# Latent attention in another order: compressed queries ahead of keys and values, V copied out in wider pieces

## The chip, the cores and the metric

The kernel runs on one core of one Trainium2 chip. The metric is device time in microseconds (us), the median over timed runs of the whole program. Five engines work side by side, each from a queue that it runs strictly in order: TensorE (PE, products; its weight loads are PEld), VectorE (DVE), ScalarE (ACT), GpSimd (POOL) and SyncE (SP, which here only issues DMAs). They meet at semaphores.

## What is computed

Two decoder layers over 512 tokens of width 1024: forgetting attention ("fox") with a feed-forward block, then multi-head latent attention ("MLA") with another. The change lies in the second attention and in how both attentions store V. Cut to what matters:

```python
def mla_shared_kv(h, positions, kv_norm, w_kv_a, ckv_norm, w_uk, w_uv):
    hn = rmsnorm(h, kv_norm)
    a = hn @ w_kv_a                                   # 1024 -> 256 + 32
    c_kv = rmsnorm(a[..., :KV_RANK], ckv_norm)
    k_rope = rope(a[..., KV_RANK:][:, :, None, :], positions)
    k_nope = jnp.einsum('bsr,rhd->bshd', c_kv, w_uk)  # 256 -> 16 heads x 64
    v = jnp.einsum('bsr,rhd->bshd', c_kv, w_uv)
    ...
def mla_attention(xn, positions, k, v, w_dq, cq_norm, w_uq, w_o):
    c_q = rmsnorm(xn @ w_dq, cq_norm)                 # 1024 -> 768
    q = (c_q @ w_uq).reshape(B, S, MLA_HEADS, MLA_NOPE + MLA_ROPE)
    q = jnp.concatenate([q[..., :MLA_NOPE], rope(q[..., MLA_NOPE:], positions)], axis=-1)
    o = causal_block_attention(q, k, v, 1.0 / math.sqrt(MLA_NOPE + MLA_ROPE))
    return o.reshape(B, S, MLA_HEADS * MLA_V) @ w_o
```

## The kernel before

Every matrix product is made to fp32 accuracy from two halves: an operand is split into a high part (ACT copies it to a rounded type) and a low part (DVE subtracts), and three products hi·hi, hi·lo, lo·hi are summed in PSUM (`mm3`, L356 to L359). Weights come by DMA into two stage buffers, and ACT (L101 or L110) and DVE (L102 or L111) split them one step ahead of use. `specs` lists the weights in the order in which `getw` asks for them; those named in `ACT_QUEUE` (`uk`, `uq`, `uv`) are loaded from ACT's queue, the rest from SP's. Activations lie with features on partitions and the 512 tokens along the free dimension; a PSUM bank holds 128 x 512.

The MLA stage (L851 on) first makes `kva` (keys' and values' compressed form, token by token, L862 to L873), then the row of inverse norms `hrow`, then six units `dq` (compressed queries, L921 to L932; after the second of them `feature_major` transposes `kro` and `ckv`, L893). L1018 to L1028 prepare the first pair of heads. A k unit is 6 products (`uk`, L941), a query unit 18 (`uq`, L968: the plain ones, L988, and the rotary one that four heads share, L1000), a v unit 24 products of 256 columns (`uv`). Before, their order is: k unit 0, first half of the rotary unit, the queries' norm row `qrow`, by which the rotary tables `rope_s` and `rope_c` are multiplied (L1023, L1024), second half, plain unit 0, `to_heads(0)`, v unit 0, plain unit 1. `to_heads` (L958) and the k unit write the heads' operands by SP's DMAs into one of three tiles `mqk`: part 0 the query's hi and lo (L966), part 3 the rotary query (L965), parts 1 and 2 the key (L955, 512 KB a head); `kr` holds the rotary key (L917).

`attention` then runs 16 heads in a pipeline: score products of the next head (L407, three passes), transposes of the probabilities (L436), softmax (L420 to L430), "fill" steps that prepare later heads, and the product with V (L450). `v_unit` (L505) holds two token blocks of V in a PSUM bank and copies each out in pieces of one block and two heads, 128 x 128, ACT the hi part (L540, fox L545), DVE the lo part (L541, fox L546).

What stands in the code is not yet the queues' order: at build time a scheduler with its own estimate of durations places the instructions on each engine, and the engines keep to it.

Of the kernel before, what the change touches and what calls it, by code (L numbers as in the profile page):

```python
# [56 lines left out]
def yoco_fox_mla_kernel(  # L57
# [152 lines left out]
    def gcol(base):  # L210
        return lambda k: gain_t[:, base + k:base + k + 1]

    G_ATTN, G_FFN, G_KV, G_CKV, G_CQ = 0, 16, 32, 40, 42

    for hf in range(2):
        spec(("kva", hf), [(0, (4, KVR + ROPE), kslice(w_kv_a, 0, KVR + ROPE, 4 * hf, 4 * hf + 4))],
             gained(4, KVR + ROPE, gcol(G_KV + 4 * hf)))
    for m in range(QT):
        spec_cols(("dq", m), mla_w_dq[0], m * P, gain=gcol(G_ATTN + 8))
# [4 lines left out]
    def spec_uk(pp):  # L224
        spec_cols(("uk", pp), uk_f, pp * P, nk=2)
# [9 lines left out]

    spec_uk(0)
    spec_uq(0)
# [267 lines left out]
    def v_unit(key, src, nk, halves, V, new_v, col, extra=None):  # L505
# [6 lines left out]
        def go(hf, ks, b):  # L512
# [21 lines left out]
            if hf == halves - 1 and (extra or off == 256):  # L534
                for bb in ([b] if extra else [b - 1, b]):
                    tt, oo = st[bb]
                    for pr in range(2):
                        pv = tt[:, oo + pr * P:oo + (pr + 1) * P].rearrange("p (h d) -> p h d", h=2)
                        if col is None:
                            ACT.copy(out=V[pr][:, bb, :, 0:64], in_=pv)  # L540
                            DVE.tensor_tensor(out=V[pr][:, bb, :, 64:128], in0=pv,  # L541
                                              in1=V[pr].bitcast(F32)[:, bb, :, 0:64], op=ALU.subtract)
                        else:
                            c = col[:, bb:bb + 1]
                            ACT.activation(out=V[pr][:, bb, :, 0:64], in_=pv, func=AF.Copy, scale=c)  # L545
                            DVE.scalar_tensor_tensor(out=V[pr][:, bb, :, 64:128], in0=pv, scalar=c,  # L546
                                                     in1=V[pr].bitcast(F32)[:, bb, :, 0:64],
                                                     op0=ALU.mult, op1=ALU.subtract)
                    if extra:
                        extra(bb, tt[:, 256:272])  # L550
# [54 lines left out]
    with ExitStack() as fx:  # L605
# [18 lines left out]
        def vtiles():  # L624
            return [fpool.tile([P, NB, 2, P], F32R, name="v", tag="v", bufs=4) for _ in range(2)]
# [112 lines left out]
        def fox_passes(n):  # L738
# [4 lines left out]
                  lambda n: (lambda kb: vts[n // 4][n // 2 % 2][:, kb, n % 2, :]), oT, fills)  # L743
# [107 lines left out]
    with ExitStack() as fx:  # L851
# [9 lines left out]

        kvb = [dense_bank() for _ in range(NB)]  # L862
        for hf in range(2):
            w = getw(("kva", hf))
            wh, wl = kview(w[0], KVR + ROPE), kview(w[1], KVR + ROPE)
            for b in range(NB):
                o = kvb[b][:, 0:KVR + ROPE]
                for i in range(4):
                    xh = xs[:, 0, 4 * hf + i, b * P:(b + 1) * P]
                    xl = xs[:, 1, 4 * hf + i, b * P:(b + 1) * P]  # L870
                    PE.matmul(o, lhsT=xh, rhs=wh[:, i, :], start=(hf == 0 and i == 0), stop=False)
                    PE.matmul(o, lhsT=xh, rhs=wl[:, i, :], start=False, stop=False)
                    PE.matmul(o, lhsT=xl, rhs=wh[:, i, :], start=False, stop=(hf == 1 and i == 3))  # L873
            if hf == 0:
                hcol = rms.finish()
        hrow = to_row(hcol)
# [16 lines left out]
        def feature_major():  # L893
# [10 lines left out]
            rope_keys(krf)  # L904

        def rope_keys(krf):
# [6 lines left out]
            krs = mp.tile([P, 2, S], F32R, name="krs", tag="rr", bufs=1)  # L913
            ACT.copy(out=krs[r, 0, :], in_=krf[r])
            DVE.tensor_tensor(out=krs[r, 1, :], in0=krf[r], in1=krs.bitcast(F32)[r, 0, :], op=ALU.subtract)
            for q in range(2):
                SP.dma_start(out=kr.bitcast(F32)[q * 64:(q + 1) * 64, :],  # L917
                             in_=krs.bitcast(F32)[r, q:q + 1, :].broadcast_to([ROPE, 2, S]))


        for m in range(QT):  # L921
            w = getw(("dq", m))
            o = dense_bank()
            dense(o, w, xs, range(KT), True, True)
            if m == 0:
                rq = Rms(QT, QR)
            if m == 1:
                feature_major()
            c = tmp_tile("cq")
            DVE.tensor_tensor(out=c, in0=o, in1=hrow, op=ALU.mult)  # L930
            gained_split(cc, m, c, gcol(G_CQ)(m))
            rq.add(c)  # L932
# [5 lines left out]
        def mbank(name):  # L938
            return bank(early.pop(0) if early else ps_mm, name)

# [59 lines left out]
        def rope_unit(qd):  # L1000
            def done(o):
                raw = tmp_tile("qr")
                ACT.copy(out=raw, in_=o)
# [15 lines left out]
        rope0 = rope_unit(0)  # L1019
        run(k_unit(0) + rope0[:1])  # L1020
        qrow = to_row(rq.finish(), -QW ** -0.5)
        state["qrow"] = qrow
        DVE.tensor_tensor(out=rope_s, in0=rope_s, in1=qrow, op=ALU.mult)  # L1023
        DVE.tensor_tensor(out=rope_c, in0=rope_c, in1=qrow, op=ALU.mult)  # L1024
        run(rope0[1:])
        run(nope_unit(0, 0))
        to_heads(0)
        run(uv_unit(0, vts[0]) + nope_unit(0, 1))  # L1028
# [143 lines left out]
```

## Time and profile before

| | us |
|---|---|
| timed runs (median of 3; lowest, highest) | 1243.5 (1242.1, 1244.34) |
| the profiled execution, its own time | 1242.24 |
| its span, first to last instruction | 1240.5 |
| TensorE busy, share of the span | 1215.9, 98% |
| VectorE busy, share of the span | 720.0, 58% |

The profile is that of one execution: its page, and views asked of its trace (stretches with each engine's busy time, engines in order of time, who waited for whom). A busy PE is read with care, since its products are pipelined: what tells is the distance from one start to the next, and the gaps. All times inside the trace count from the span's start.

### The profile page before, as it was taken

The numbers are of one execution on the slowest core, as the hardware profiler recorded it, in microseconds if no ns is written. First come the engines' busy times: TensorE is split into PE (matmuls) and PEld (weight loads), VectorE is DVE, ScalarE is ACT, GpSimd is POOL, SyncE is SP. The second block draws the span as 40 slices with busy tenths as digits, with TensorE's granted clock in tenths as the row PEclk, the third lists the DMA queues.
The fourth block names the chain that finished last, engine by engine and source line by source line (L and its number), as shares of the span: only waits on it lengthen the run. The fifth ranks groups of instructions, "written<-read, shape, count | busy, mean of one in ns | idle before, by whom it ended". The sixth has DMA issues, their size and how long they took to land. (4 is left out here: it accounts for less than half of the span.)

```text
span 1240.5 us, 16569 instructions
## 1 busy us (share of the span) xinstructions
PE 1215.9 (98%) x5963; PEld 1023.5 (83%) x5963; DVE 720.0 (58%) x1525; ACT 537.8 (43%) x1188; POOL 245.1 (20%) x277
## 2 busy tenths in 40 slices
PE   8999999999999999999999899999999999999997
PEld 7878888888888888888898788888888888888886
DVE  5776777755455545633367789876545455552323
ACT  6555565543323323323364467665423333232322
POOL 3333332211111111000012133333011111110101
PEclk9999999999999999999999999999999999999999
DMA  5555455142332333333324675634233323332232
GB/s 173 142 144 140 115 129 136 52 118 86 102 101 87 102 95 90 104 106 95 102 86 105 155 186 147 167 102 135 85 100 88 102 85 102 89 98 102 85 104 84
DMA packets 193396, 137.24 MB, mean 111 GB/s; under 512 B 5937, under 2 KB 174945, under 8 KB 193313
## 3 DMA queue, kind: packets, MB, share of 16 engines
q1 hardware_dynamic: 186208, 128.55, 37.7%
q10 hardware_dynamic: 7104, 7.63, 2.1%
q8 instruction: 47, 0.77, 0.3%
q14 instruction: 37, 0.30, 0.1%
HBM read 104.30 MB, written 2.10 MB: 86 GB/s over the span
## 5 line engine op out<-in xcount | busy, mean ns | idle before, releaser
L101 ACT CAST whi<-wstage 128x512 fp32r<-128x512 f32 (+4 forms) x386 | 215.7, 603 | 464.5 <-PE dn L358 296.7
L102 DVE TENSOR_TENSOR wlo<-wstage,whi 128x512 fp32r<-128x512 f32 x366 | 282.6, 806 | 117.6 <-ACT whi L101 117.4
L357 PE MATMUL dn<-xs,whi 128*128 128x512 f32 x704 | 275.0, 391 | 0.0
L359 PE MATMUL dn<-xs,wlo 128*128 128x512 f32 x704 | 274.1, 389 | 0.0
L358 PE MATMUL dn<-xs,whi 128*128 128x512 f32 x704 | 274.0, 389 | 0.0
L359 PEld LDWEIGHTS dn<-xs,wlo 128*128 128x128 f32 x704 | 132.2, 188 | 27.4
L357 PEld LDWEIGHTS dn<-xs,whi 128*128 128x128 f32 x704 | 132.2, 188 | 27.2
L358 PEld LDWEIGHTS dn<-xs,whi 128*128 128x128 f32 x704 | 132.2, 188 | 27.1
L781 POOL TENSOR_TENSOR u<-u,g 128x512 f32<-128x512 f32 x44 | 68.7, 1562 | 425.0 <-DVE u L780 379.6
L780 DVE TENSOR_TENSOR u<-dn,inv_row 128x512 f32<-128x512 f32 x44 | 30.4, 691 | 146.8 <-PE dn L359 146.8
L427 POOL TENSOR_SCALAR p<-p,rs 128x128 f32<-128x128 f32 (+1 forms) x128 | 63.8, 507 | 136.1 <-DVE rs L424 134.3
L422 ACT ACTIVATE p<-s,nm 128x256 f32<-128x256 f32 (+3 forms) x128 | 67.4, 544 | 22.1 <-DVE nm L420 19.2
L420 DVE CUSTOM_DVE_ANT_0 s<-s,mask 128x256 f32<-128x256 f32 (+3 forms) x128 | 61.1, 495 | 16.1 <-PE s L407 16.1
L777 DVE TENSOR_TENSOR g<-dn,inv_row 128x512 f32<-128x512 f32 x44 | 30.4, 691 | 68.8 <-PE dn L359 68.8
L321 POOL TENSOR_TENSOR acc<-acc,sq 128x512 f32<-128x512 f32 x22 | 35.4, 1610 | 161.8 <-ACT sq L320 161.7
L441 DVE TENSOR_TENSOR pt<-t,pt 128x384 fp32r<-128x384 f32 (+1 forms) x96 | 52.6, 591 | 3.3 <-ACT pt L440 2.5
L440 ACT CAST pt<-t 128x384 fp32r<-128x384 f32 (+1 forms) x96 | 45.0, 524 | 18.5 <-PE t L436 17.2
L436 PE MATMUL t<-ident,p 128*128 128x128 f32 x320 | 44.6, 275 | 6.9 <-DVE oraw L454 6.6
L357 PE MATMUL qkp<-xs_fox,whi 128*128 128x512 f32 x128 | 51.2, 400 | 0.0
L358 PE MATMUL qkp<-xs_fox,whi 128*128 128x512 f32 x128 | 50.3, 393 | 0.0
L436 PEld LDWEIGHTS t<-ident,p 128*128 128x128 f32 x320 | 36.4, 140 | 16.8 <-DVE oraw L454 9.0
L359 PE MATMUL qkp<-xs_fox,wlo 128*128 128x512 f32 x128 | 50.1, 392 | 0.0
(290 smaller groups left out, 2346.7 us busy)
## 6 DMA issues: line engine op xcount, KB each, us to landing
wstage<-in_w_gate SPq DMA_DIRECT2D x44, 512.0 KB
wstage<-in_w_up SPq DMA_DIRECT2D x44, 512.0 KB
wstage<-in_w_down SPq DMA_DIRECT2D x30, 512.0 KB
wstage<-in_fox_w_in SPq DMA_DIRECT2D x22, 512.0 KB
qk<-hl SPq DMA_DIRECT2D x32, 256.0 KB
mqk<-hl SPq DMA_DIRECT2D x16, 512.0 KB
wstage<-in_w_down SPq DMA_DIRECT2D x16, 448.0 KB
wstage<-in_mla_w_uq ACTq DMA_DIRECT2D x8, 576.0 KB
```

Source lines behind the costliest of these rows:

```text
L101: ACT.copy(out=hi[:, a:b], in_=stage[:, a:b])
L102: (POOL if shared and a else DVE).tensor_tensor(out=lo[:, a:b], in0=stage[:, a:b], in1=hi.bitcast(F32)[:, a:b], op=ALU.subtract)
L357: PE.matmul(o, lhsT=wh, rhs=xh, start=start, stop=False)
L358: PE.matmul(o, lhsT=wh, rhs=xl, start=False, stop=False)
L359: PE.matmul(o, lhsT=wl, rhs=xh, start=False, stop=stop)
L420: DVE.tensor_tensor_reduce(out=sv, in0=sv, in1=mask[:, S - n:S], scale=1.0, scalar=BIG, op0=ALU.add, op1=ALU.min, accum_out=nm[:, qb:qb + 1])
L422: ACT.activation(out=pv, in_=sv, func=AF.Exp, bias=nm[:, qb:qb + 1], scale=-1.0, accum_out=ssum[:, qb:qb + 1])
L427: POOL.tensor_scalar(out=pv[:, :cut], in0=pv[:, :cut], scalar1=r, scalar2=1.0, op0=ALU.mult, op1=ALU.mult)
L436: PE.transpose(t[:, i * P:(i + 1) * P], self.p[:, POFF[qb] + kb * P:POFF[qb] + (kb + 1) * P], ident)
L440: ACT.copy(out=self.pt[0][:, sl], in_=t[:, :n])
L441: DVE.tensor_tensor(out=self.pt[1][:, sl], in0=t[:, :n], in1=self.pt[0].bitcast(F32)[:, sl], op=ALU.subtract)
L781: POOL.tensor_tensor(out=u, in0=u, in1=g, op=ALU.mult)
```

## The change

Five edits. (1) The six `dq` units come ahead of `kva`; the first two wait for `hrow` and are copied out together. (2) The queries' norm is taken between the halves of `kva`, and its row `qrow` behind them. (3) The first plain unit and the rotary unit come next, then `to_heads(0)`, then `feature_major`, the second plain unit, the k unit and the v unit. The rotary unit of the first four heads multiplies by `qrow` itself; the tables are multiplied by `qrow` later (`rope_rows`), behind the rotary key, for the other units. (4) The hi and lo of the rotary key lie in two tiles of the `tmp` pool. (5) V is copied out in pieces of 256 columns: in MLA two token blocks of two heads, in fox one block of four heads, whose tile now holds four heads.

```diff
+    for m in range(QT):
+        spec_cols(("dq", m), mla_w_dq[0], m * P, gain=gcol(G_ATTN + 8))
     for hf in range(2):
         spec(("kva", hf), ...
-    for m in range(QT):
-        spec_cols(("dq", m), mla_w_dq[0], m * P, gain=gcol(G_ATTN + 8))
...
+    spec_uq(0)
     spec_uk(0)
-    spec_uq(0)
     spec_uv(0)
...
+                if col is None:
+                    for pr in range(2):
+                        pv = t.rearrange("p (b r h d) -> p r b h d", b=2, r=2, h=2)[:, pr]
+                        bs = slice(b - 1, b + 1)
+                        ACT.copy(out=V[pr][:, bs, :, 0:64], in_=pv)
+                        DVE.tensor_tensor(out=V[pr][:, bs, :, 64:128], in0=pv,
+                                          in1=V[pr].bitcast(F32)[:, bs, :, 0:64], op=ALU.subtract)
...
+            rope_rows()
+
+        def rope_rows():
+            DVE.tensor_tensor(out=rope_s, in0=rope_s, in1=state["qrow"], op=ALU.mult)
+            DVE.tensor_tensor(out=rope_c, in0=rope_c, in1=state["qrow"], op=ALU.mult)
...
-        rope0 = rope_unit(0)
-        run(k_unit(0) + rope0[:1])
-        qrow = to_row(rq.finish(), -QW ** -0.5)
-        state["qrow"] = qrow
-        DVE.tensor_tensor(out=rope_s, in0=rope_s, in1=qrow, op=ALU.mult)
-        DVE.tensor_tensor(out=rope_c, in0=rope_c, in1=qrow, op=ALU.mult)
-        run(rope0[1:])
-        run(nope_unit(0, 0))
+        run(nope_unit(0, 0) + rope_unit(0))
         to_heads(0)
-        run(uv_unit(0, vts[0]) + nope_unit(0, 1))
+        feature_major()
+        run(nope_unit(0, 1) + k_unit(0) + uv_unit(0, vts[0]))
```

The queues that this makes differ most just ahead of the first head's scores. On VectorE, before, from the rotary product by `rope_c` (L1007) to the second plain query (the last `qf`); `rr` is the rotary query, `mv` V, `wlo` the low half of a weight, here of later units:

```order
L1007 TENSOR_TENSOR qr<-qr,rope_c 128x512
L993 TENSOR_TENSOR qf<-uq,inv_row 128x512
L1008 TENSOR_TENSOR qr<-qr,sw 128x512
L996 TENSOR_TENSOR hl<-qf,hl 128x512
L1011 TENSOR_TENSOR rr<-qr,rr 128x512
L541 TENSOR_TENSOR mv<-vv,mv 128x2x64
L102 TENSOR_TENSOR wlo<-wstage,whi 128x256
L541 TENSOR_TENSOR mv<-vv,mv 128x2x64 x4
L102 TENSOR_TENSOR wlo<-wstage,whi 128x512
L541 TENSOR_TENSOR mv<-vv,mv 128x2x64 x2
L993 TENSOR_TENSOR qf<-uq,inv_row 128x512
```

And now, from the rotary key's product (`krf`) to the first copies of V; `hl<-uk,hl` is the low half of the first key, the 128x512 piece of `wlo` that of `uv`'s weights:

```order
L939 TENSOR_TENSOR krf<-krf,rope_c 32x512
L1030 TENSOR_TENSOR rr<-qr,rr 128x512
L940 TENSOR_TENSOR krf<-krf,sw 32x512
L931 TENSOR_TENSOR rope_s<-rope_s,inv_row 128x512
L932 TENSOR_TENSOR rope_c<-rope_c,inv_row 128x512
L943 TENSOR_TENSOR krs<-krf,krs 32x512
L1009 TENSOR_TENSOR qf<-uq,inv_row 128x512
L102 TENSOR_TENSOR wlo<-wstage,whi 128x512
L102 TENSOR_TENSOR wlo<-wstage,whi 128x256
L1012 TENSOR_TENSOR hl<-qf,hl 128x512
L966 TENSOR_TENSOR hl<-uk,hl 128x512
L541 TENSOR_TENSOR mv<-vv,mv 128x4x64 x3
```

What moved: the key's low half, before done long ago, is now the last of eleven rows that begin with the rotary key, and the split of `uv`'s weights stands behind the second plain query.

The rows of VectorE just ahead of these, now, from the rotary query's product by `qrow` (`qr<-uq`):

```order
L1020 TENSOR_TENSOR qr<-uq,inv_row 128x512
L1024 STREAM_SHUFFLE sw<-qr 128x512
L937 STREAM_SHUFFLE sw<-krf 32x512
L1026 TENSOR_TENSOR qr<-qr,rope_c 128x512
L377 SCALAR_TENSOR_TENSOR cc<-ct,gain_t,cc 128x512
L1027 TENSOR_TENSOR qr<-qr,sw 128x512
L377 SCALAR_TENSOR_TENSOR cc<-ct,gain_t,cc 128x512
```

Rotary query, rotary key and the compressed keys (`cc<-ct`) now take turns here; before, the last two were done between the `dq` units.

SP's queue of DMAs up to the first head, before:

```order
L917 DMA kr<-krs 64x1x512 x2
L955 DMA mqk_5398<-hl 128x1x1024
L955 DMA mqk_5399<-hl 128x1x1024
L966 DMA mqk_5398<-hl 128x1x512
L965 DMA mqk_5398<-rr 64x1x512 x2
L965 DMA mqk_5399<-rr 64x1x512 x2
```

and now:

```order
L982 DMA mqk_5370<-hl 128x1x512
L982 DMA mqk_5371<-hl 128x1x512
L981 DMA mqk_5370<-rr 64x1x512 x2
L981 DMA mqk_5371<-rr 64x1x512 x2
L945 DMA kr<-krs 64x1x512 x2
L981 DMA mqk_5372<-rr 64x1x512
L971 DMA mqk_5370<-hl 128x1x1024
L971 DMA mqk_5371<-hl 128x1x1024
```

What moved: the key's copies (1024 columns) went from ahead of the query's to behind them and behind `kr`.

## Rows read from the trace of the kernel before

**Rows 1.** The page: busy time, share of the span and instructions of TensorE.

```profile
PE 1215.9 (98%) x5963; PEld 1023.5 (83%) x5963; DVE 720.0 (58%) x1525; ACT 537.8 (43%) x1188; POOL 245.1 (20%) x277
```

**Rows 2.** Stretches: length, busy time per engine, PE clock (1.00 full), DMA share, GB/s.

```profile
679.00:686.00 7.00, 7.00 (x46) 6.28 (x45) 5.86 (x9) 2.29 (x5) 1.67 (x1) 1.00 0.60 176
...
689.30:692.60 3.30, 0.36 (x3) 0.18 (x3) 0.68 (x1) 0.39 (x1) 0.00 (x0) 1.00 1.05 319
692.60:695.80 3.20, 3.20 (x11) 2.91 (x12) 1.75 (x7) 2.34 (x7) 0.00 (x0) 0.51 0.44 110
695.80:700.00 4.20, 4.20 (x22) 3.43 (x21) 2.96 (x14) 2.13 (x8) 2.10 (x4) 0.97 0.42 93
```

**Rows 3.** PE in order of time: start, duration, instruction, [idle before <- releaser].

```profile
689.14 0.51 PE L407 MATMUL s<-mqk 128*128 128x256 f32 x2
692.58 0.47 PE L407 MATMUL s<-kr,mqk 128*128 128x256 f32 x1 [2.94 <-DMA mqk<-rr]
692.85 0.63 PE L407 MATMUL s<-mqk 128*128 128x256 f32 x2
693.28 0.41 PE L407 MATMUL s<-kr,mqk 128*128 128x256 f32 x1
...
695.74 0.56 PE L357 MATMUL uk<-cc,whi 128*128 128x512 f32 x1
```

**Rows 4.** Waits of PE, 600 to 860 us: total, times, longest.

```profile
PE s L407 <- DMA mqk<-rr: 2.9, 1, 2.9
PE t L436 <- DVE oraw L454: 1.8, 2, 0.9
PE uk L357 <- DVE mv L541: 1.6, 2, 0.8
PE o L450 <- DVE pt L441: 1.2, 1, 1.2
```

**Rows 5.** PE in order of time, a query unit's end and the v unit.

```profile
681.65 0.39 PE L358 MATMUL uq<-cc,whi 128*128 128x512 f32 x1
681.88 0.39 PE L359 MATMUL uq<-cc,wlo 128*128 128x512 f32 x1
682.11 0.28 PE L531 MATMUL vv<-whi,cc 128*128 128x256 f32 x1
682.22 0.28 PE L532 MATMUL vv<-wlo,cc 128*128 128x256 f32 x1
...
684.98 0.40 PE L357 MATMUL uq<-cc,whi 128*128 128x512 f32 x1
```

**Rows 6.** DVE in order of time.

```profile
680.41 0.69 DVE L1023 TENSOR_TENSOR rope_s<-rope_s,inv_row 128x512 f32<-128x512 f32 x1 [1.02 <-ACT inv_row L352]
681.02 0.68 DVE L1024 TENSOR_TENSOR rope_c<-rope_c,inv_row 128x512 f32<-128x512 f32 x1
681.74 1.67 DVE L1007 TENSOR_TENSOR qr<-qr,rope_c 128x512 f32<-128x512 f32 x1
...
686.10 0.41 DVE L102 TENSOR_TENSOR wlo<-wstage,whi 128x256 fp32r<-128x256 f32 x1
```

**Rows 7.** POOL in order of time: the rotary products.

```profile
650.10 1.29 POOL L910 TENSOR_TENSOR sw<-sw,rope_s 32x512 f32<-32x512 f32 x1 [6.54 <-DVE sw L909]
...
681.18 1.67 POOL L1006 TENSOR_TENSOR sw<-sw,rope_s 128x512 f32<-128x512 f32 x1 [11.72 <-DVE rope_s L1023]
```

**Rows 8.** SP and ACT in order of time: DMA issues.

```profile
685.41 0.52 SPq L966 DMA_DIRECT2D mqk<-hl  x1
686.03 1.29 SPq L965 DMA_DIRECT2D mqk<-rr  x2
...
686.55 0.37 ACTq L137 DMA_DIRECT2D wstage<-in_mla_w_uq  x1
```

**Rows 9.** Stretches around DMAs: columns as in rows 2.

```profile
676.00:679.00 3.00, 3.00 (x15) 2.45 (x14) 2.66 (x15) 0.59 (x1) 0.00 (x0) 1.00 1.00 180
...
685.40:686.50 1.10, 1.10 (x6) 0.89 (x6) 1.10 (x3) 0.61 (x4) 0.00 (x0) 1.00 0.00 0
...
688.50:691.00 2.50, 1.14 (x6) 0.58 (x4) 1.23 (x4) 0.47 (x2) 0.00 (x0) 1.00 0.98 325
```

**Rows 10.** Copies of MLA's V: count, duration in ns (lowest/median/highest).

```profile
L541 DVE TENSOR_TENSOR mv<-vv,mv x32: 271/282/292, 685.9 to 812.9; 128x128 fp32r<-128x128 f32 x32
```

**Rows 11.** Waits of PE, 0 to 270 us (the fox attention): total, times, longest.

```profile
PE t L436 <- DVE oraw L454: 4.8, 8, 0.9
```

More of the change, by code (lines that the diff above doesn't have):

```diff
@@ L534, in go @@
             if hf == halves - 1 and (extra or off == 256):
-                for bb in ([b] if extra else [b - 1, b]):
-                    tt, oo = st[bb]
[L537 to L548, printed above, removed]
+                if col is None:
[5 more added lines that the diff above has]
+                                          in1=V[pr].bitcast(F32)[:, bs, :, 0:64], op=ALU.subtract)
+                for bb in ([] if col is None else [b] if extra else [b - 1, b]):
+                    tt, oo = st[bb]
+                    pv = tt[:, oo:oo + 256].rearrange("p (h d) -> p h d", h=4)
+                    c = col[:, bb:bb + 1]
+                    ACT.activation(out=V[0][:, bb, :, 0:64], in_=pv, func=AF.Copy, scale=c)
+                    DVE.scalar_tensor_tensor(out=V[0][:, bb, :, 64:128], in0=pv, scalar=c,
+                                             in1=V[0].bitcast(F32)[:, bb, :, 0:64],
+                                             op0=ALU.mult, op1=ALU.subtract)
                     if extra:
@@ L624, in vtiles @@
         def vtiles():
-            return [fpool.tile([P, NB, 2, P], F32R, name="v", tag="v", bufs=4) for _ in range(2)]
+            return [fpool.tile([P, NB, 4, P], F32R, name="v", tag="v", bufs=2)]
         def decay_rows(dst, head):
@@ L742, in yoco_fox_mla_kernel @@
         attention(att, FOX_PAIRS, fox_passes,
-                  lambda n: (lambda kb: vts[n // 4][n // 2 % 2][:, kb, n % 2, :]), oT, fills)
+                  lambda n: (lambda kb: vts[n // 4][0][:, kb, n % 4, :]), oT, fills)
     def out_proj(prefix, oT, opened, ks, gain):
@@ L859, in mvt @@
             return [mp.tile([P, NB, 2, P], F32R, name="mv", tag="mv", bufs=3) for _ in range(2)]
+        pend = []
+        for m in range(QT):
+            w = getw(("dq", m))
+            o = dense_bank()
+            dense(o, w, xs, range(KT), True, True)
+            pend.append((m, o))
+            if m == 0:
+                hcol = rms.finish()
+                continue
+            if m == 1:
+                hrow = to_row(hcol)
+                rq = Rms(QT, QR)
+            for mm, oo in pend:
+                c = tmp_tile("cq")
+                DVE.tensor_tensor(out=c, in0=oo, in1=hrow, op=ALU.mult)
+                gained_split(cc, mm, c, gcol(G_CQ)(mm))
+                rq.add(c)
+            pend = []
         kvb = [dense_bank() for _ in range(NB)]
@@ L874, in yoco_fox_mla_kernel @@
             if hf == 0:
-                hcol = rms.finish()
-        hrow = to_row(hcol)
+                qcol = rq.finish()
+        qrow = to_row(qcol, -QW ** -0.5)
         cf = mp.tile([P, 2, S], F32, name="ckv", tag="hl", bufs=3)
@@ L912, in rope_keys @@
             DVE.tensor_tensor(out=krf[r], in0=krf[r], in1=sw[r], op=ALU.add)
-            krs = mp.tile([P, 2, S], F32R, name="krs", tag="rr", bufs=1)
-            ACT.copy(out=krs[r, 0, :], in_=krf[r])
-            DVE.tensor_tensor(out=krs[r, 1, :], in0=krf[r], in1=krs.bitcast(F32)[r, 0, :], op=ALU.subtract)
+            krs = [tmp.tile([P, 1, S], F32R, name="krs", tag="tmp") for _ in range(2)]
+            ACT.copy(out=krs[0][r, 0, :], in_=krf[r])
+            DVE.tensor_tensor(out=krs[1][r, 0, :], in0=krf[r], in1=krs[0].bitcast(F32)[r, 0, :], op=ALU.subtract)
             for q in range(2):
                 SP.dma_start(out=kr.bitcast(F32)[q * 64:(q + 1) * 64, :],
[L918 to L932, printed above, removed]
+                             in_=krs[q].bitcast(F32)[r].broadcast_to([ROPE, 2, S]))
         state = {}
@@ L939, in mbank @@
             return bank(early.pop(0) if early else ps_mm, name)
+        state["qrow"] = qrow
         def k_unit(pp):
@@ L1002, in done @@
                 raw = tmp_tile("qr")
-                ACT.copy(out=raw, in_=o)
+                if qd == 0:
+                    DVE.tensor_tensor(out=raw, in0=o, in1=state["qrow"], op=ALU.mult)
+                else:
+                    ACT.copy(out=raw, in_=o)
                 sw = tmp_tile("sw")
```

## The prediction

> **What bounds the kernel now.** I began with the busy times: TensorE has 1215.9 us of work in a span of 1240.5 [rows 1], so only its gaps can be gained or lost. Next came PE in order of time around the first latent head. PE runs without a pause up to 689.1, does one score pass at 689.14, and then waits 2.94 us, to 692.58, for the rotary query's DMA [rows 3]. Behind that wait the granted clock is 0.51, the lower of two levels (1.2 of 2.4 GHz), until about 695.8; then 0.97 again [rows 2]. So a wait here costs its own length and slows what follows. The rest of the latent attention has five short waits: 1.8 us for the head's output before the transposes, 1.6 for V's copies, 1.2 for transposed probabilities [rows 4]. That is all an edit here can give back; the question is what it does to 692.58.
>
> **PE's own work** is the same. Products start 0.227 us apart at 512 columns (681.65, 681.88, 682.11) and half of that at 256; the v unit takes 684.98 − 682.11 = 2.87 [rows 5]. So the k unit's 6 products are 1.36, a query unit's 18 are 4.08; the twelve transposes I put at 1.2. In the new order PE has nothing to wait for until the v unit, so I count back from 689.1, where the same work ends: v unit from 686.25, k unit 684.9, second plain unit 680.8, transposes 679.6, rotary unit 675.5 to 679.6.
>
> **VectorE behind the rotary unit** is the main term. Before, the key was copied long ahead, and the last thing the first head needed was the rotary query. Now its first key is the last of 18 rows on DVE that begin when the rotary unit ends, at 679.65 (the 7 and the 11 rows quoted with the change). A 128x512 product starts 0.61 after the one ahead of it (680.41, 681.02), a 256-column split takes 0.41 in all, 0.35 to the next [rows 6]. I give every other row 0.6 to 0.67 (the 32-row ones too, an upper estimate): 4.45 + 6.35 = 10.8, plus the tail of the last: the key's low half is done at 690.6 if nothing holds DVE.
>
> Something does. The rotary product by `rope_c` took 1.67 against 0.68 of its neighbour [rows 6], while POOL's product of `sw` ran (681.18 for 1.67) [rows 7]. Both rotary products now fall into these 18 rows: +1.0 for the query's, and for the key's (1.29 on POOL [rows 7]) between +0.4, what overlaps a product already under way, and +1.0. I take 692.0 for the key's low half; bounds 690.6 (both POOL products beside shuffles and work that reads PSUM) and 692.7.
>
> **The split of `uv`'s weights**, fifteenth of these rows, is ready at 689.0 to 690.4, where the v unit wants it with its second product at 686.4. PE will idle there 2.5 to 4 us and end the v unit at about 693. That costs nothing of its own, since scores wait for the key until later still; it is the price if the key should come early, and it puts the lower clock ahead of the scores.
>
> **SP's queue.** The key's two copies (512 KB) are issued when the low half is done; ahead of them stand only the copies of `kr` and rotary queries, whose data is older by several rows. How long from issue to landing? Before, the four copies of the first two heads' queries, also 512 KB in all, were issued from 685.41; the second rotary pair has 686.03 + 0.6 = 686.6 [rows 8], and landed at 692.58 [rows 3]: 5.9 from the last issue, 7.2 from the first. No byte moved for 1.1 us, and at 688.5 to 691.0 traffic ran at 325 GB/s, much of it `uq` weights [rows 9] that ACT issued at 686.55 [rows 8]. The key's copies themselves ran at 180 GB/s (676 to 679) [rows 9], so alone they would need 1.1 + 2.9 = 4.0. In the new order ACT issues the next `uq` weights right behind the key's high half, so the competition stays: I take 5.9. The key lands at 692.0 + 5.9 = 697.9; bounds 690.6 + 4.0 = 694.6 and 692.7 + 7.2 = 699.9.
>
> **What that does to PE.** The first score product waits for the key, so the first pass that ran at 689.14 now comes behind the wait too: two 256-column passes at the lower clock are +0.43, the spacing of such a pass there (693.28 − 692.85) [rows 3]. One key product of the next unit is already done (−0.4, an estimate: somewhat under twice its 0.227 at the full clock). The slow clock lasts as long as before. The shift is 697.9 − 692.58 = **+5.3** (bounds +2.0 and +7.3).
>
> **What is given back.** The attention starts later, while DVE's work runs on, so its queue is further ahead. The 1.2 for `pt` falls in the first head, where DVE then has some microseconds more: **−1.1** (−1.2 to 0). V's copies: 32 pieces of 0.282 [rows 10] are 9.0; 16 of the double width, at the 0.41 of a 256-column split [rows 6], are 6.6, and all four of a v unit stand ahead of the output's copies. The two waits for `mv` of 0.8 [rows 4] lose what one piece holds each: **−1.2** (−1.6 to 0). The 1.8 before the transposes hangs on a chain through the softmax that no edit shortens: 0 (−1.8 to 0).
>
> **Fox.** The same widening there makes half as many copies of twice the width. PE waits in fox for the output's copy (4.8 us, 8 times) [rows 11], never for V, so I put 0; between −1.5, if shorter copies on DVE free a third of that, and +1.0, if a piece of double length stands ahead of an output copy (0.28 against 0.41 [rows 6, 10], 8 times). The separate tiles of the rotary key, and the tables multiplied later, are inside the 18 rows.
>
> **Sum.** +5.3 − 1.1 − 1.2 + 0 + 0 = +3.0. The profiled execution took 1242.24, so it would become 1245.2; it lies 1.3 below the median of 1243.5, to which the same shift gives **1246.5**. With all bounds on one side the sum reaches from −4.1 to +8.3.
>
> **Rivals.** *The key behind the weights.* If the `uq` weights get their bytes first, as the query copies suffered before (7.2 from the first issue [rows 3, 8]), the key lands at 692.0 + 7.2 = 699.2, +6.6. With only the 1.1 given back: +5.5, **1249.0**, slower. For it: the weights move in that very stretch at 325 GB/s [rows 9]. Against: ACT issues them behind the key's own high half, so most of the key is queued first.
>
> *The attention pays it back: not slower.* The mechanism is DVE's lead. If the copies of V in wide pieces and a later start remove all short waits in the latent attention (1.2 + 1.6 + 1.8 [rows 4]) and a sixth of fox's 4.8 [rows 11] (0.8), 5.4 comes back. With the key at 696.5 (+3.9), half a microsecond behind a quiet copy (692.0 + 4.0 = 696.0), the sum is −1.5: **1242.0**. It decides once the waits given back exceed the delay of the key, some 4 us. For it: all these waits are for DVE. Against: the 1.8 is chained to the softmax, not to V.
>
> *The copy is quick.* The traffic of 325 GB/s [rows 9] could all belong to the key: 1.1 to the first byte, 1.6 for 512 KB, 0.5 for the second issue [rows 8] make 3.2; with 692.0 the key lands at 695.2, +2.6, and with −2.3 given back the sum is +0.3: **1243.8**, no measurable change. Against: the nearest row for copies out of `hl` is 180 GB/s [rows 9], and the queries took 5.9.
>
> The Trainium skill has such a rule, "DMA: Bandwidth & Descriptors", section "Anatomy of one DMA — SWDGE (gpsimd) path": a fixed 2.0 us plus the bytes at 436 GB/s, fitted on copies that GpSimd issued. By it the key's 512 KB would take 3.2 us (an estimate), and the sum would be this rival's. The queries' 5.9 us for as many bytes disagrees, so I keep it a rival.
>
> **How the numbers follow.** A measurement of this kernel can tell about 0.2%, 2.5 us, from no change, so "same" is 1241.0 to 1246.0. Forecast (0.55): 1246.5, with 1244.5 to 1248.5 as its own range; 0.33 slower, 0.22 same. Key behind the weights (0.18): slower. Paid back (0.15): 0.08 faster, 0.07 same. Quick copy (0.12): 0.02 faster, 0.09 same, 0.01 slower. Together: faster 0.10, same 0.38, slower 0.52. For 8 in 10 the range reaches from the paid-back case at 1242.0 to 1250.0, one above the heavier one; the outer bounds (−4.1, +8.3) need every term at its end and stay out.
>
> **What would show it.** Right: PE waits 2.5 to 4 us near 686.5 in the v unit for DVE's split of `uv`'s weights, and then 3 to 6 us for the key's DMA, the first full score pass at about 698 in place of 692.58; clock near 0.5 behind it; the rotary product on DVE at more than 1 us beside POOL; no waits left for `mv`. Wrong: the key's low half done before 689; a first score pass before 695; a wait for the key's DMA that starts after the rotary query landed and ends within 4 us of its issue; or new waits in the later heads or in fox of more than 2 us in all, which would overturn the parts I put at nothing.

## The result, and the profile after

The changed kernel took 1252.12 us (median; 1251.85 to 1252.6), the kernel before 1242.95 on the same chip: ratio 1.0073, interval 1.0056 to 1.0091. It is slower by 9.2 us. The forecast was slower, by 3.0 us, with a range to 1250.0: the sign was right, the size was three times too small.

TensorE's busy time is nearly the same as in [rows 1]; the page of the changed kernel:

```profile
span 1250.1 us, 16498 instructions
...
PE 1219.8 (98%) x5963; PEld 1025.2 (82%) x5963; DVE 722.4 (58%) x1494; ACT 533.0 (43%) x1155; POOL 241.3 (19%) x277
```

So the 9.6 us by which the span grew are in waits, and in products at the lower clock. The waits of PE between 560 and 900 us (total, times, longest), which answer to [rows 4]:

```profile
PE vv L532 <- DVE wlo L102: 3.8, 1, 3.8
PE s L407 <- DMA mqk<-hl: 3.4, 1, 3.4
PE t L436 <- DVE oraw L454: 1.5, 2, 0.7
PE uq L359 <- DVE wlo L102: 1.0, 2, 0.6
PE o L450 <- DVE pt L441: 0.7, 2, 0.4
PE s L407 <- ACT p L422: 0.5, 1, 0.5
```

Both waits that the prediction named are there: the v unit for the split of `uv`'s weights, and the first scores for the key's DMA. The same place on PE in order of time, which answers to [rows 3]:

```profile
688.72 0.40 PE L531 MATMUL vv<-whi,cc 128*128 128x256 f32 x2
692.95 0.58 PE L532 MATMUL vv<-wlo,cc 128*128 128x256 f32 x1 [3.84 <-DVE wlo L102]
693.33 0.41 PE L533 MATMUL vv<-whi,cc 128*128 128x256 f32 x1
...
697.81 0.63 PE L357 MATMUL uk<-cc,whi 128*128 128x512 f32 x1
701.86 0.67 PE L407 MATMUL s<-mqk 128*128 128x256 f32 x2 [3.42 <-DMA mqk<-hl]
702.32 0.42 PE L407 MATMUL s<-kr,mqk 128*128 128x256 f32 x1
```

And the stretches around it (columns as in [rows 2]), where the clock is the column of 0.85, 0.50, 0.89 and 0.52:

```profile
688.80:693.00 4.20, 0.36 (x4) 0.16 (x2) 4.20 (x8) 1.29 (x3) 0.00 (x0) 0.85 0.48 108
693.00:697.80 4.80, 4.80 (x22) 4.80 (x23) 2.29 (x5) 1.18 (x3) 0.00 (x0) 0.50 0.96 245
697.80:702.20 4.40, 0.98 (x4) 0.50 (x4) 2.05 (x4) 1.98 (x5) 0.00 (x0) 0.89 1.00 231
702.20:705.50 3.30, 3.30 (x13) 3.02 (x13) 0.98 (x4) 0.00 (x0) 0.00 (x0) 0.52 0.99 263
```

Read downward: PE stands for 3.8 us while VectorE is busy without a gap (4.20 of 4.20); then the v unit runs wholly at the lower clock (0.50; 4.8 us, where [rows 5] had 2.87); then PE stands again, now with the DMA engines full (1.00); and the first scores run at the lower clock, as they did before.

To compare traces I took the start of the same numbered product in each and subtracted that of before. For the changed kernel this gives four parts: **+1.35** by the first fox products (the first tokens arrive later), **+1.0** in the first fox v unit, **+7.4** up to the first full score pass (702.32 − 2.37 = 699.95 against 692.58), and **−0.1** from there to the last product. Together 9.6. The first part can't be laid to the change: over the fourteen traces of this study it lies between −0.2 and +1.8, in kernels with and without each edit, and the trace of before is the second lowest of them.

### The profile page after: what moved, and what is told of

The parts are those of the page before. It is cut to its first block, busy times and chain, and to the rows that moved or that the text cites. A ratio compares the mean times of both kernels' runs of the same rounds, so it can differ in the third digit from the quotient of the medians.

```text
span 1250.1 us, 16498 instructions
## 1 busy us (share of the span) xinstructions
PE 1219.8 (98%) x5963; PEld 1025.2 (82%) x5963; DVE 722.4 (58%) x1494; ACT 533.0 (43%) x1155; POOL 241.3 (19%) x277
## 4 chain that ended last, share of the span: by engine, by line
PE 88%; DVE 5%; DMA 4%; ACT 2%; issue 1%; SPq 0%; POOL 0%; ACTq 0%; DVEq 0%; POOLq 0%
PE dn L357 18%; PE dn L358 18%; PE dn L359 18%; PE dn L1117 3%; PE dn L1116 3%; PE dn L1115 3%; PE s L407 3%; PE o L450 2%; PE t L436 2%; PE qkp L358 2%; PE qkp L357 2%; PE qkp L359 2%; PE vv L532 1%; PE vv L531 1%; PE vv L533 1%; DVE hl L649 1%
## 5 line engine op out<-in xcount | busy, mean ns | idle before, releaser
L101 ACT CAST whi<-wstage 128x512 fp32r<-128x512 f32 (+4 forms) x386 | 214.9, 602 | 469.8 <-PE dn L358 280.6
L422 ACT ACTIVATE p<-s,nm 128x384 f32<-128x384 f32 (+3 forms) x128 | 67.5, 545 | 23.2 <-DVE nm L420 18.9
L420 DVE CUSTOM_DVE_ANT_0 s<-s,mask 128x128 f32<-128x128 f32 (+3 forms) x128 | 61.2, 496 | 17.1 <-PE s L407 16.7
```

Source lines behind the costliest of these rows:

```text
L101: ACT.copy(out=hi[:, a:b], in_=stage[:, a:b])
L420: DVE.tensor_tensor_reduce(out=sv, in0=sv, in1=mask[:, S - n:S], scale=1.0, scalar=BIG, op0=ALU.add, op1=ALU.min, accum_out=nm[:, qb:qb + 1])
L422: ACT.activation(out=pv, in_=sv, func=AF.Exp, bias=nm[:, qb:qb + 1], scale=-1.0, accum_out=ssum[:, qb:qb + 1])
```

## The experiments

The table gathers what the runs below showed. "Key" is the time from the issue of the first head's key copy to the first score product (a landing where PE waited for it, else an upper bound); "first pass" and "rest" are the shifts against before, up to the first full score pass (the start and fox taken out) and from there to the end. The last four columns are read from one trace each, and parts of 1 or 2 us are finer than the timed runs resolve: the intervals of the change, e1, e3 and e6 overlap widely.

| run | ratio to before (interval) | key | fox | first pass | rest |
|---|---|---|---|---|---|
| the change | 1.0073 (1.0056, 1.0091) | 7.4 | +1.0 | +7.4 | −0.1 |
| e1 narrow V | 1.0066 (1.0040, 1.0091) | 6.9 | 0 | +7.2 | +2.2 |
| e2 wide V alone | 0.9994 (0.9981, 1.0007) | | +0.9 | +0.2 | −0.1 |
| e3 weights behind key | 1.0085 (1.0055, 1.0116) | at most 4.7 | 0 | +4.6 | +6.1 |
| e4 key first | 1.0050 (1.0037, 1.0063) | 7.6 | 0 | +6.3 | −0.2 |
| e5 one key copy | a single run, 1252.32 us | 7.2 | +1.0 | +6.9 | +0.5 |
| e6 fox narrow | 1.0065 (1.0049, 1.0080) | 7.0 | 0 | +6.8 | +0.4 |
| e7 rotary unit first | 1.0022 (1.0013, 1.0031) | 8.9 | +0.9 | +5.0 | −3.0 |
| e8 the same, lean | 1.0026 (1.0017, 1.0036) | 8.2 | 0 | +4.7 | −2.2 |
| e9 early weights | 1.0030 (1.0019, 1.0041) | at most 5.9 | 0 | +5.6 | −3.2 |
| e10 early weights, on before | 1.0030 (1.0018, 1.0042) | | 0 | −2.4 | +4.8 |
| e11 weights behind, on before | 1.0021 (1.0009, 1.0033) | | 0 | −2.2 | +5.6 |
| e12 e8 and e9 together | 0.9988 (0.9978, 0.9998) | 6.2 | 0 | +2.7 | −3.0 |

"First pass" and "rest" are to be added: +7.3 for the change, +2.4 for e9, +2.5 for e8, +2.0 for e7, −0.3 for e12. In e9 "rest" is −3.2 because eight products of later units (six `uk`, two `uq`) stood ahead of the scores and the scores ran at the full clock. In e7, e8 and e12 none did; there it is for the most part short waits that are gone. Waits of PE behind the first pass came to 4.6 us before [rows 4]; in e7 this one is left:

```profile
PE t L436 <- DVE oraw L454: 0.9, 1, 0.9
```

In e8 they sum to 2.7, in e12 to 2.0. In the changed kernel it is 3.7 (the list above).

### V's pieces: e1, e2, e6

e1 takes the changed order and gives V its old narrow pieces, in both attentions.

```diff
-                        pv = t.rearrange("p (b r h d) -> p r b h d", b=2, r=2, h=2)[:, pr]
-                        ACT.copy(out=V[pr][:, bs, :, 0:64], in_=pv)
+                        pv = tt[:, oo + pr * P:oo + (pr + 1) * P].rearrange("p (h d) -> p h d", h=2)
+                        ACT.copy(out=V[pr][:, bb, :, 0:64], in_=pv)
```

> The changed order with V copied out in the old narrow pieces (edit 5 undone in both attentions). Theory A (the loss lies in four places: +7.3 us at the first latent head, +1.0 in fox because the first query copy of VectorE stands behind six small rows when V's pieces are wide, +1.35 in the arrival of the first tokens, nothing given back in the latent attention): fox's +1.0 is gone, the first latent score stays 7.3 us late, the two waits of 0.8 us for mv are back but the waits that took their place are gone, so about 1 us less than the changed kernel: 1250 to 1251.5. Rival B (the wide pieces cost more than that, in the latent attention too): under 1249. Rival C (they gained something there): 1252 or more.

It took 1252.43. Fox's +1.0 is gone, the first score as late as in the changed kernel, but the rest is 2.2 us longer, since the waits for V's copies are back and one of them has grown (waits of PE from 700 us on):

```profile
PE uk L357 <- DVE mv L541: 3.4, 2, 2.6
PE s L407 <- DMA mqk<-hl: 3.4, 1, 3.4
PE t L436 <- DVE oraw L454: 1.5, 2, 0.8
```

The wait of 2.6 stands right behind the first scores, and PE comes out of it at a lower clock (0.65 granted from 706 to 710.4 us). So in these traces the wide pieces are worth 2.3 us to the latent attention of the new order, a wait and the clock behind it (1.8 by e6's trace, below). That is rival C, where theory A had nothing given back. e2 is the other half, the kernel before with wide pieces alone (the diff above with its signs turned, and the same for fox).

> The kernel before with V copied out in wide pieces (edit 5 alone). Theory A: +1.0 in fox, the first latent score at its old place relative to that, the waits for mv gone and others of like size in their place: 1243.5 to 1245. Rival B: 1246 or more. Rival C (the waits for mv are truly saved, fox unharmed): 1241.5 or less.

It is the same as before (0.9994), as theory A had it. The two waits for `mv` of [rows 4] are gone, and yet the rest is only 0.1 us shorter. Its waits of PE from 700 us on:

```profile
PE t L436 <- DVE oraw L454: 1.5, 2, 0.7
PE o L450 <- DVE pt L441: 0.9, 3, 0.4
```

In sum they are 2.2 us less: 1.6 for `mv`, 0.3 for `oraw`, 0.3 for `pt`; by the distances from start to start behind the slow stretch, which also hold gaps that this view does not name, 1.3 less. What took it back is the clock behind the first scores. It stays low until 699.4, where in the kernel before it was up again by 696 [rows 2]:

```profile
693.80:697.00 3.20, 3.15 (x10) 2.98 (x11) 0.85 (x3) 1.66 (x4) 0.00 (x0) 0.50 0.61 160
697.00:699.40 2.40, 2.40 (x7) 1.83 (x6) 2.27 (x11) 1.82 (x8) 0.58 (x2) 0.50 0.29 68
```

PE had waited 3.4 us for the rotary query there (2.94 before). That this is what keeps the clock down longer is argued from the two traces, not tested. e6 leaves the wide pieces to the latent attention alone.

```diff
-                    pv = tt[:, oo:oo + 256].rearrange("p (h d) -> p h d", h=4)
+                    for pr in range(2):
+                        pv = tt[:, oo + pr * P:oo + (pr + 1) * P].rearrange("p (h d) -> p h d", h=2)
```

> The changed kernel with fox's V in the old narrow pieces and the latent attention's in the wide ones. Theory A: the first fox v unit waits no longer for the query copy, fox's +1.0 us is gone; the first latent head is as late as in the changed kernel and the latent attention as there: 1250.5 to 1251.5, 1 us under the changed kernel. Rival (the +1.0 has another cause than the widths, such as the start): 1252.

1250.31, and fox's +1.0 is gone from the trace (the ratios, 1.0065 and 1.0073, don't tell the two kernels apart). What it was can be seen on VectorE. In the changed kernel the first query copy (`qf`, L646) stands behind six small rows of the forget gate; with narrow pieces it stands behind two. The changed kernel, with PE's wait for that copy on top, then e9, which has the same order there and no such wait:

```profile
PE vv L531 <- DVE qf L646: 0.8, 1, 0.8
```

```profile
39.49 2.60 DVE L689 SCALAR_TENSOR_TENSOR fw<-fw,fw 128x64 f32<-128x64 f32 x6
42.07 0.69 DVE L646 TENSOR_TENSOR qf<-qkp,inv_row 128x512 f32<-128x512 f32 x1
```

```profile
38.64 1.52 DVE L698 SCALAR_TENSOR_TENSOR fw<-fw,fw 128x64 f32<-128x64 f32 x6
40.15 0.69 DVE L655 TENSOR_TENSOR qf<-qkp,inv_row 128x512 f32<-128x512 f32 x1
```

The same six rows take 2.60 or 1.52: there is one pause among the small rows in every trace, at a slightly different row, of 1.0 to 1.1 us in eleven traces and 0.4 to 0.6 in e3, e4 and e9. In four kernels with the wide pieces (the change, e2, e5, e7) it falls ahead of `qf`, and PE waits; in three (e3, e4, e9) behind it, and PE does not. So the +1.0 came only where both met, the order and a pause ahead of `qf`; what the pause is stays open, and with it how often the +1.0 comes.

### The key's DMA: e3, e5, e9

The prediction put the landing at 5.9 us from the issue. It was 7.4 (694.46 to 701.86). DMA issues of SP and ACT in the changed kernel:

```profile
694.46 1.20 SPq L971 DMA_DIRECT2D mqk<-hl  x2
```

```profile
692.98 0.38 ACTq L137 DMA_DIRECT2D wstage<-in_mla_w_uq  x1
```

ACT issues 576 KB of query weights 1.5 us ahead of the key. e3 holds both halves of these weights until the first two heads' keys have landed.

```diff
+            for j, t in enumerate(behind if late else []):
+                POOL.tensor_copy(out=st[:, j:j + 1], in_=t.bitcast(F32)[:, 2, 0:1])
+            (ACT if specs[i][0][0] in ACT_QUEUE and not late else SP).dma_start(out=dst, in_=src)
```

> The changed kernel, with the loads of the next query weights made to wait for the first key's copies (a tiny copy by GpSimd from the landed keys into the stage buffer ahead of each load, loads on SyncE's queue). Theory A (the key's copies took 7.4 us because 576 KB of weights shared the DMA engines): the key lands 4 to 5 us after its issue, the first score comes 2.5 to 3.5 us earlier than in the changed kernel; what the later weights cost behind it can eat that up, so the time is 1249 to 1254 and only the landing decides. Rival D (the copy has this pace by itself, by its two issues and its shape): 7 us or more again, first score within 0.5 us of its place.

The first score came 4.7 us after the issue (693.86), and PE did not even wait for the key there:

```profile
698.57 0.47 PE L411 MATMUL s<-mqk 128*128 128x256 f32 x2
```

That is theory A's landing, and 2.8 us earlier than in the changed kernel. As expected the weights then come late ("PE uq L361 <- ACT whi L101", 4.2 us), and the time is no better (1.0085, an interval that holds the change's 1.0073). e5 tests the bytes of the key itself, which the prediction had halved: it wrote 512 KB for both copies, and each copy is 512 KB.

```diff
+                    if pp == 0 and hb == 1:
+                        continue
                     SP.dma_start(out=dst[:, 1:3, :], in_=src)
```

> The changed kernel, in which the second head's first key copy (512 KB) is left out of the stretch ahead of the first scores (that half of the tile is filled earlier, from other data, so head 1 computes something else); everything else keeps its order. In the changed kernel the first head's key landed 7.4 us after its issue, with two copies of 512 KB and the query weights (576 KB) under way; with the weights held back 4.7. Theory G (the bytes: the prediction counted 512 KB for both copies, they are 1 MB): landing 1 to 2.5 us sooner, 5 to 6.4 us after its issue, and the first score as much earlier relative to the v unit's end. Rival (the weights alone, queued on the same engines, set the landing): 7 us or more.

Theory G fell. With the second copy gone, the first lands as late as with it:

```profile
701.81 0.50 PE L407 MATMUL s<-mqk 128*128 128x256 f32 x2 [3.22 <-DMA mqk<-hl]
```

694.60 to 701.81 is 7.2 us. So the second copy's bytes are not what delays the first. The run does not show that bytes behind the key cost nothing at all, since ACT's second half of the weights moved up into their place (0.81 MB of weights by the landing, 0.64 in the changed kernel).

What did pass ahead of the key can be read from the packets by DMA queue: q1 carries SP's copies, q10 ACT's loads (from 655 to 706 us q10 moves 2.80 MB in the changed kernel and 1.25 in e9, where the weights are loaded at another time or by SP). Packets, MB and share of the 16 engines in the first 2 us behind the key's issue, the changed kernel (694.46 to 696.46), then e3 (693.86 to 695.86):

```profile
q10 hardware_dynamic: 275, 0.42, 68.7%
q1 hardware_dynamic: 48, 0.07, 20.8%
```

```profile
q1 hardware_dynamic: 157, 0.36, 75.3%
```

SP's queue nearly stands while the 576 KB pass that ACT issued 1.5 us ahead; in the kernel before it stood the same way ahead of the rotary query (688.4 to 690.4: 0.09 MB against 0.49 on q10). The second half of the weights, issued by ACT 1.3 us behind the key (695.78), moved 0.02 MB from 698.46 to 701.46, so it is the first half that the key stood behind, though e3 and e9 hold both back. e9 takes the weights out of the way and makes only their second half late (PE then waits 1.8 us for its split): the first half is loaded some 67 us earlier (issued at 624.20 to 625.14; 20 were expected) into one of V's tiles, still free then, and the second waits for the landed key.

```diff
+        loaded["uq", 1, 0] = [wq[:, 0:512], wq[:, 512:1024], wt]
+        ACT.dma_start(out=wq[:, 0:768].rearrange("p (a b) -> p a b", b=4 * QW),
+                      in_=kslice(mla_w_uq[0], 4 * QW, 8 * QW, 0, 2))
...
+            late = specs[i][0] == ("uq", 1, 1)
```

> The changed kernel in which the next query weights don't move while the first key does: their first half (576 KB) is loaded some 20 us earlier into memory that is free then (three loads), their second half waits for the first key to have landed. Nothing is late for PE by that. Theory A (weights that ACT issues 1.5 us ahead of the key go through the DMA engines first, and that costs the key 2.7 us): key landed 4.7 us after its issue, first score 2.5 to 3 us earlier relative to the v unit's end, 1248.5 to 1250. Rival (the early loads only move the traffic onto the weights of the units before, or the net is nothing): 1251.5 or more.

1246.3 (1.0030 against the change's 1.0073), more than theory A had it. PE waits for the split of `uv` as in the changed kernel, but no longer for the key, and the clock is full again when the scores begin:

```profile
690.98 0.58 PE L541 MATMUL vv<-wlo,cc 128*128 128x256 f32 x1 [3.84 <-DVE wlo L103]
...
698.41 0.40 PE L416 MATMUL s<-mqk 128*128 128x256 f32 x2
698.64 0.28 PE L416 MATMUL s<-kr,mqk 128*128 128x256 f32 x1
```

```profile
694.00:698.00 4.00, 3.49 (x17) 2.94 (x17) 2.40 (x6) 1.81 (x5) 0.18 (x1) 0.77 1.01 217
698.00:702.00 4.00, 4.00 (x22) 3.49 (x23) 3.07 (x13) 1.95 (x7) 0.72 (x3) 1.00 0.95 219
```

The last pass above takes 0.28, where the changed kernel's takes 0.42: besides the wait, the scores get their clock back, which the expectation had left out.

### VectorE's queue: e4, e7, e8

e4 puts the key unit ahead of the second plain query unit.

```diff
-        run(nope_unit(0, 1) + k_unit(0) + uv_unit(0, vts[0]))
+        run(k_unit(0) + nope_unit(0, 1) + uv_unit(0, vts[0]))
```

> The changed kernel with the first key unit ahead of the second plain query unit. On VectorE the key's low half then stands ahead of three rows (a plain query's two and 256 columns of a weight's split, 0.6 + 0.35 + 0.6 = 1.55 us). Theory A (the DVE queue sets the key): key issued 1.5 us earlier, first score 1.5 us earlier, 1250 to 1251. Rival E (the landing is set by the weights' traffic that is issued in that stretch, not by the key's issue): first score at the same place within 0.5 us, 1252. Rival F (V's weights, now split later still, push the v unit past the key's landing): first score waits for PE's own v unit, 1252 or more.

The key is issued 1.4 us earlier, the first pass comes 1.1 earlier, as theory A had it. The time, 1249.47, is half a microsecond below its range; fox's +1.0 was absent in this trace, so part of that is luck. The wait for `uv`'s split shrank to 1.6, that for the key grew to 5.6; both are the same lateness seen at two places. e7 changes the order more: rotary unit first, key unit right behind the transposes.

```diff
-        run(nope_unit(0, 0) + rope_unit(0))
+        run(rope_unit(0) + nope_unit(0, 0))
         to_heads(0)
         feature_major()
-        run(nope_unit(0, 1) + k_unit(0) + uv_unit(0, vts[0]))
+        run(k_unit(0) + nope_unit(0, 1) + uv_unit(0, vts[0]))
```

> The changed kernel with the first three units in another order: rotary unit, first plain unit, transposes, k unit, second plain unit, v unit. The rotary query's five rows on VectorE then run while PE does the plain unit, and only the key's rows are left behind the transposes; the key's low half stands ahead of the second plain query. Theory A (the loss is VectorE's queue in the last 7 us of PE's cover): the key's low half is done 5 to 7 us earlier than in the changed kernel, the first full score pass comes 5 to 8 us earlier, about 1243 to 1246 (fox's +1.0 stays). Rival E (the DMA traffic sets it whatever VectorE does): under 3 us earlier, 1249 or more.

1245.01, theory A's time, but not by its path. 5 to 7 us were wanted for the key's low half, and it came 4.0 earlier; the first pass came 2.4 earlier, which is rival E's "under 3". The rest is 2.9 shorter: of the short waits only the 0.9 shown above is left. The key now took 8.9 us from its issue (690.78), and that is the only long wait ("PE s L407 <- DMA mqk<-hl", 6.8 us). The stretches show why: the DMA engines are full from 686 on (share 0.94, 0.88, 1.04).

```profile
686.00:690.00 4.00, 4.00 (x20) 3.32 (x19) 4.00 (x7) 1.93 (x4) 0.35 (x1) 1.00 0.94 218
690.00:694.00 4.00, 2.83 (x24) 2.62 (x22) 3.44 (x8) 1.61 (x4) 0.00 (x0) 1.00 0.88 248
694.00:698.00 4.00, 0.00 (x0) 0.00 (x0) 0.39 (x1) 1.04 (x2) 0.00 (x0) 0.64 1.04 248
```

e8 is e7 with `rope_rows()` called behind the last line and fox in narrow pieces.

> The order of the run before (rotary unit first), and in addition the two products of the rotary tables taken behind the v unit, and fox's V in narrow pieces: a candidate to beat both kernels. Theory A: the key's low half one more row earlier, its copy issued near 685 (in the time of the kernel before), landed near 690; PE waits about 1 us or less for the first score in place of 2.94, and fox's +1.0 is gone: 1238.5 to 1242. Rival (the waits only move: scores start earlier, but the latent attention's short waits grow by as much): 1242 to 1244. Rival E: 1247 or more.

1245.14, no better than e7. The expected landing near 690 was far off: the key's low half was ready at 687.1 in the time of before (the first key product waited 0.9 for ACT's copy of `cc`), and the copy took 8.2 us. Both theories were wrong on the size; the queue on VectorE and the traffic are in series, and shortening one lengthens the other.

### The same on the kernel before: e10, e11, and both kernels beaten: e12

e10 is e9's edit on the kernel before, the second half of the weights behind the landed rotary query.

> The same edit on the kernel before: first half of the next query weights loaded early, second half behind the landed rotary query. There 512 KB of query copies took 5.9 us from their last issue, while 576 KB of weights moved in the same stretch. Theory A: the rotary query lands 1.5 to 3 us earlier, the wait of 2.94 us ahead of the first full score pass is cut to 0 to 1.4 us, 1238.5 to 1241.5: better than both kernels. Rival H (the wait then goes to another DMA or to the first softmax): 1242 to 1244.

The rotary query did land 2.4 us earlier (690.19 in the time of before), the first pass ran at the full clock, and the kernel was slower (1246.08). The gain went into a new wait of 3.2 for the second half of the weights and a longer one for V's copies (2.5 us, 1.6 before):

```profile
691.08 0.35 PE L416 MATMUL s<-kr,mqk 128*128 128x256 f32 x1 [0.74 <-DMA mqk<-rr]
...
705.54 0.51 PE L366 MATMUL uq<-cc,whi 128*128 128x512 f32 x1 [3.17 <-ACT whi L102]
```

That is rival H, and more than it had. e11 holds back the first half only and loads nothing early (the diff of e3 with the key `("uq", 1, 0)` and part 3 of the tile).

> The kernel before, first half of the next query weights held back until the first head's rotary query has landed, nothing loaded early. Theory A: the rotary query lands as early as in the run before this one, but the weights come 2 to 3 us later, and the query unit behind the first scores waits for their split: 1241 to 1245. Rival (weights aren't what delays the rotary query): the first full score pass within 0.5 us of 692.6.

1245.12, the upper end of theory A: first pass 2.2 us earlier, then 2.7 us for the late weights and 2.5 for `pt` (1.2 before). e12 puts e9's early weights on e8's order.

> The order with the rotary unit first, late rotary tables and fox in narrow pieces, and the early weights on top. In that order the key was issued 6 us earlier than in the changed kernel but landed 8.2 us after its issue, behind the copies of rotary queries and rotary key and the weights. Theory A (DMA traffic of that stretch is the bound: 576 KB at 200 to 300 GB/s less is 2 to 3 us): key landed 2 to 3 us earlier, 1242 to 1243.5. Rival (the copies of rotary queries and keys ahead of it on the same queue are the bound): within 1 us of the run without the early weights, 1244 to 1245.5.

1241.54 against 1241.98, ratio 0.9988 (0.9978 to 0.9998): at best 0.2% faster than the kernel before, an interval that just leaves out 1, and by the two ratios 0.8% faster than the changed one. The key landed 6.2 us after its issue, 2.0 less than in e8; PE still waits for it:

```profile
693.36 1.86 PE L416 MATMUL s<-mqk 128*128 128x256 f32 x5 [3.26 <-DMA mqk<-hl]
```

## Why the prediction was wrong, point by point

**PE's cover, right.** The v unit was to wait near 686.5; its second product was ready to start at about 689.0 − 2.4 = 686.6, and the wait of 3.84 is inside the 2.5 to 4 us. The v unit was said to end at 693 and ended at 697.8 − 2.4 = 695.4, because it ran at the lower clock; the prediction put that clock "ahead of the scores" and gave it no time.

**VectorE's 18 rows, right in the sum, in part by luck.** The low half was predicted at 692.0 and done at 694.43 − 2.37 = 692.06. The rows of the changed kernel, from the first to the last:

```profile
681.80 0.69 DVE L1020 TENSOR_TENSOR qr<-uq,inv_row 128x512 f32<-128x512 f32 x1 [2.02 <-PE uq L359]
...
685.67 1.76 DVE L1027 TENSOR_TENSOR qr<-qr,sw 128x512 f32<-128x512 f32 x1 [0.53 <-POOL sw L1025]
...
692.23 1.00 DVE L102 TENSOR_TENSOR wlo<-wstage,whi 128x512 fp32r<-128x512 f32 x2
...
693.76 0.67 DVE L966 TENSOR_TENSOR hl<-uk,hl 128x512 fp32r<-128x512 f32 x1
```

681.80 to 694.43 is 12.63 where 12.35 was forecast (679.65 to 692.0). But neither row that was to be held was: `qr<-qr,rope_c` took 0.66 beside GpSimd's product (its forecast sign was more than 1 us), `krf<-krf,rope_c` 0.67. Another was, `qr<-qr,sw` (1.76), which ran beside GpSimd's product for the key, after 0.53 of waiting for that for the query; its 1.1 and the 0.5 come to 1.6 where 1.4 was put on the other two:

```profile
683.42 2.22 POOL L1025 TENSOR_TENSOR sw<-sw,rope_s 128x512 f32<-128x512 f32 x1 [4.32 <-DVE sw L1024]
685.60 1.28 POOL L938 TENSOR_TENSOR sw<-sw,rope_s 32x512 f32<-32x512 f32 x1
```

**The key's DMA, the first step that failed.** Taken 5.9, measured 7.4; with 0.1 from VectorE's rows that is 1.6 us at the landing (701.86 − 2.37 = 699.5 against 697.9). The prediction's first rival had 699.2 for "the key behind the weights", and that is what happened. The argument against it, that ACT issues the weights behind the key's own high half and so most of the key is queued first, mixed up two queues: the weights follow ACT's row, the key's copies follow VectorE's last row and then SP's own earlier copies, 1.5 us later. e3 and the packets by queue show the price of the weights; e5 shows that the key's second copy costs the first 0.2 us at most. The row that the 5.9 came from held such a stop itself: without the weights the queries landed 2.4 and 2.2 us sooner (e10, e11). The halved byte counts were an error too, but not the one that made the difference (the key's copies are 512 KB each, and the query copies are 512 KB a head, 256 and two of 128, so 1 MB for two). By the rule cited there from the Trainium skill ("DMA: Bandwidth & Descriptors", "Anatomy of one DMA — SWDGE (gpsimd) path") 512 KB take 3.2 us (an estimate), and 1 MB 4.4 (an estimate). The trace does not agree with it while the weights pass. With the weights away the first copy took at most 4.7 (e3), with them 7.4; so 3.2 is not ruled out for a copy alone; no run here had the engines wholly empty.

**What is given back, the second.** −2.3 was summed, −0.1 came; with the other small differences behind the first score that is 2.6 us in all. The step took each short wait by itself. The waits for `mv` did go, as the count of pieces said (16 pieces of 0.424, predicted 0.41), but new ones stand in the list above: 1.0 for the split of the late weights, 0.5 for the softmax, and gaps without a name. With the 0.8 in fox that is 2.3 us of new waits, over the 2 that the prediction named as its own sign of being wrong here. The wait for `pt` (−1.1) shrank by 0.5; the softmax chain, put at 0, gave 0.3. Where the first three units come in another order (e7) the short waits do go, 3.7 of 4.6 us; why they stay in the changed kernel is not tested.

**Fox, the third.** Put at 0, measured +1.0, the upper bound. Its cause was not the one named (a long piece ahead of an output copy) but the order of the first query copy on VectorE, which the prediction had left out, together with the pause. That it came out at the bound is chance: the change's trace has it, e3, e4 and e9 with the same wide pieces do not.

**The start.** +1.35 in the one profiled execution, within what the start does from trace to trace.

3.0 + 1.6 + 2.6 + 1.0 + 1.4 = 9.6, the span's growth. Of the rivals the first was right on the mechanism and nearer on what comes back (it kept 1.1, nearly nothing came); its 1249.0 lacked that, fox and the start. The quick copy and the paid-back attention fell for this change, though e7, e8 and e12 show 2 to 3 us paid back in other orders.

## What to carry to other kernels

When a step is moved behind others, list for each engine *and for the DMA engines* what now stands ahead of it in order of issue, with its bytes: here the key's copy left a place some 13 us ahead of the first scores (issued from 675.58 in the trace of before) for one right behind 576 KB of weights, in a stretch in which the DMA engines were full for some 10 us, with only the v unit left to cover it. Two queues in series (VectorE's rows, then the transfers) have to be shortened together: e8 and e9 each leave some 2.5 us to before, e12 with both closes the gap. And a wait that disappears from a list of waits is a gain only if the end moves: in e2, e10 and e11 other waits or a lower clock took its place.

## What the runs showed that was not expected

- In these kernels a copy on SP's queue was held by loads issued shortly ahead of it on ACT's: 7.4 us with 576 KB ahead, 7.2 with the 512 KB behind it left out, at most 4.7 with the weights held back; for 2 us SP's queue moved 0.07 MB and ACT's 0.42.
- A pause of 1.0 to 1.1 us (in three traces about half of it) among VectorE's small rows near 40 us, at a place that differs from kernel to kernel; it goes with 1 us lost on PE or nothing by whether the row that PE waits for stands behind it or ahead.
- The first tokens' arrival differed by up to 2.0 us between traces, as much as many an edit is worth, so the shifts above are counted from behind it.
